# Order of steps in a hybrid attention, Mamba-2 and MLP block: outer SSM groups, one tile's transposes, the fifth up-projection unit

## The chip, the cores and the metric

The kernel runs on one core of a Trainium2 chip. The metric is the device time of one execution in microseconds; lower is better. The kernel before has a median of 1081.7 us in 3 runs (1081.41 to 1081.86).

## The reference

One decoder layer on 512 tokens of width 1024, all in float32. Cut to what matters:

```python
u = rmsnorm(h, norm_mix_pre_w)
q, k, v, z, xbc, dt_raw, gate_logits = split(u @ w_in)
att = dilated_attention(q, k, v) @ w_att_proj          # three (window, dilation) patterns, mixed
xs, bm, cm = split(silu(causal_conv4(xbc)))            # 8 groups of 256 channels, state 128
y = ssd_chunked(xs, dt, a, bm, cm) + d_skip * xs       # chunks of 128 tokens
y = group_rmsnorm(y * silu(z)) * ssm_norm_w            # one norm for each of the 8 groups
ssm = y @ w_ssm_proj
mixed = (sigmoid(g_att) * att + sigmoid(g_ssm) * ssm) @ w_out
h = h + rmsnorm(mixed, norm_mix_post_w)
f = square(relu(rmsnorm(h, norm_ffn_pre_w) @ w_up)) @ w_down    # hidden width 4096
h = h + rmsnorm(f, norm_ffn_post_w)
```

## The kernel before

Each float32 operand of a large product is split into a high part (`wh`, `uh`, `hh`, rounded for the matmul) and a low part (`wl`, `ul`, `hl`, the rest). ScalarE (ACT) makes the high part and VectorE (DVE) the low part. A product is then a triple of matmuls: high by high, high by low, low by high. Weights come in units of 1 MB (`ws_...`, two buffers), which the SP queue loads; a unit's load waits until the last reader of an older unit in the same buffer is done.

The order on TensorE (PE) is the order in which the program writes its matmuls. On the other engines a planner at build time sets the order by its own clock and by priorities; an instruction that is pinned stays behind the one written just before it on its engine. The planner's order is fixed in the program that runs.

**SSM groups.** The eight groups run one after the other (the loop at L923). The generator `ssm_group` (L791) has steps that hang together by short chains on several engines. In this order they are: scaling of the rows `xd` and `xs`; the products `pb` and `pcb` and the decays `w`, which DVE multiplies with `cbm`; the chunk states `pst` and `prev`; the outputs `pyd` and `pyo` with the gate, giving `y` and its square `sq`; the norm's sums `pn`, from which GpSimd (POOL) makes the power `rt` and sends it through DRAM (`rt_d`) back as a broadcast `rg`, and with which the next group's decays `w` are fetched; and the scaling of `y` by `rg`, split into `yth` and `ytl`, which the next projection reads (`pssp`). So that PE has work while these chains run, a `Filler` (L479) writes pieces of the large projections between the steps. One piece is one triple of 512 columns and counts 3 x 512 / 2400 = 0.64. The tuples `SSM_FIRST` (group 0), `SSM_FILL` (groups 1 to 6) and `SSM_LAST` (group 7) give the budget ahead of each of the seven steps; the sixth step is empty. What is overspent is taken from the next budget. The filling is a queue of units. In group 0 these are the attention projection, then `x` and `bc` of group 1. In groups 1 to 6 they are `z` of the group, the projection of the group before, then `x` and `bc` of the next group. In group 7 they are `z`, projection 6, and the gate units `gs1` to `gs3`; after these comes projection 7. When a unit's half (8 triples) ends, its evacuation is written with priority; for `x` of groups 1 to 7 that includes eight DMAs on the POOL queue, `x_d`, four for each half, and then `xd`.

**Output projection.** `out_right(i, j)` (L1013) is the second half of the output projection for token tile i: 4 triples for each of two halves j of the contraction, and after the second half `add_normed`, which gives the residual `hres`. `f_norm(i)` norms it into `fn`, and `f_transpose(i)` (L1029) transposes it on PE (`ft`) and splits it into `fh` and `fl`, which the up projection `up_first` reads.

**Up projection.** The first four units of 256 columns are plain products. Units 4 to 15 (the loop at L1245) are made by a Winograd form of Strassen's scheme: seven products of half size, with sums of the activations (`S1` to `S4`) and of the weights (`T1` to `T4`). The products are written in the order X (`A11`,`B11`), the previous unit's X (`S3`,`T3`), Y (`A12`,`B21`), the previous unit's Z (`S4`,`B22`), the previous unit's X (`A22`,`T4`), Z (`S1`,`T1`), X (`S2`,`T2`); each is 12 matmuls of 256 columns. `copy` moves a bank out on ACT (`usX`, `usY`, `usZ`), `c_sum` adds on DVE. The weight parts are split by `split_w` (L1170): ACT first, and the function that it returns does the DVE part. `b1_parts(j + 1)` splits `B11` and `B21` of the next unit (1024 columns), `b22_parts` splits `B22` (512 columns), `t12_parts` and `t34_parts` the sums, which `t_sums` (L1190) makes from the raw weights in `tt`. In the trace these tiles are `wh_wina`, `wl_wina` (for `B11`, `B21`, `T1`, `T2`) and `wh_winb`, `wl_winb` (`T3`, `T4`, `B22`). `load_up(j + 2)` (L1133) loads the raw weights of the unit after the next into the buffer of unit j. The fifth unit of the up projection is j = 4, where no previous unit of this kind exists; there the branch `else` splits `T3` and `T4`, `S3`, and `B22` of unit 4.

Of the kernel before, what the change touches and what calls it, by code (L numbers as in the profile page):

```python
# [42 lines left out]
BIG = 1e30  # L43

FILL0, FILL1, FILLA, FILLB, FILLC = 3.0, 4.0, 3.0, 2.8, 2.8
SSM_FIRST = (1, 5, 4, 3, 11, 5, 4.5)
SSM_FILL = (6, 4, 4, 4, 10, 5, 4.5)
SSM_LAST = (5, 6, 4, 4, 9, 8, 8)

V_ORDER = tuple((d, i) for d in (1, 0, 2) for i in range(NT))  # L50
V_STEPS = {(1, 0, 2): (("s", 2),), (1, 0, 5): (("t", 1),), (1, 0, 6): (("n", 2),), (1, 1, 1): (("s", 3),),
# [33 lines left out]
def hybrid_block(ctx: ExitStack, tc: tile.TileContext, a: dict):  # L85
# [77 lines left out]
    def v3(t, k):  # L163
        return t.rearrange("p (k n) -> p k n", k=k)
# [59 lines left out]
    def pin(ins):  # L224
        return tc.keep_in_program_order(ins)
# [4 lines left out]
    def tr(dst, src):  # L230
        tc.keep_in_program_order(pe.transpose(dst, src, ident))
# [4 lines left out]
    def three(ps, wh, wl, uh, ul, start, stop, w_moving=False):  # L236
        if w_moving:
            mm(ps, uh, wh, start=start, stop=False)
            mm(ps, uh, wl, start=False, stop=False)
            mm(ps, ul, wh, start=False, stop=stop)  # L240
        else:
            mm(ps, wh, uh, start=start, stop=False)
            mm(ps, wh, ul, start=False, stop=False)
            mm(ps, wl, uh, start=False, stop=stop)
# [11 lines left out]
    def gbank(name):  # L256
        return psg.tile([P, T], F32, name=name, tag="g")

    def abank(name):
        return psa.tile([P, T], F32, name=name, tag="a")  # L260
# [18 lines left out]
    with tc.tile_pool(name="start", bufs=1, reuse_waits="tile") as st:  # L279
# [7 lines left out]
        raw = st.tile([P, NT, SH], F32, name="dtraw")  # L287
# [341 lines left out]
    for key in ATT_UNITS:  # L629
        n, j = key[:-1], int(key[-1])  # L630
# [292 lines left out]
    for g in range(GROUPS):  # L923
        steps = ssm_group(g, szs[g])
        fill.through(f"bc{g}")
        for n, us in enumerate(SSM_FIRST if g == 0 else SSM_LAST if g == GROUPS - 1 else SSM_FILL):
            fill.run(us)
# [25 lines left out]
    w23 = []  # L953
    for j in range(2):
# [4 lines left out]
        lo = ow.tile([P, UF], F32R, name=f"wl_o{2 + j}", tag=f"ol{j}")  # L959
# [20 lines left out]
    def add_normed(i, pss, row, dst, at, parts=((0, T), (T, D))):  # L980

        ts_ = []
        for b in range(2):
            cs = slice(b * T, (b + 1) * T)
            jk = rp.tile([P, T], F32, name=f"jk{at}{i}_{b}", tag="jk", bufs=1)
            act.activation(jk, pss[b], AF.Square, scale=RD, accum_out=sm[:, at + b, i : i + 1])
            if b == 1:
                rstd_of(sm[:, at, i : i + 1], sm[:, at, i : i + 1], sm[:, at + 1, i : i + 1])
            t = rp.tile([P, T], F32, name=f"t{at}{i}_{b}", tag="jf", bufs=2)
            dve.tensor_tensor(t, pss[b], row[:, cs], op=ALU.mult)  # L990
            ts_.append(t)
        for c0, c1 in parts:
            tv = ts_[c0 // T][:, c0 % T : c0 % T + c1 - c0]
            dve.scalar_tensor_tensor(dst[:, c0:c1], tv, sm[:, at, i : i + 1], hres[:, i, c0:c1],
                                     op0=ALU.mult, op1=ALU.add)

    def out_part(ps, i, j, w, ks=range(4)):

        for k in ks:
            o = 4 * j + k  # L1000
            three(ps, v3(w[0], 4)[:, k, :], v3(w[1], 4)[:, k, :], mix[o][0][:, i * P : (i + 1) * P],
                  mix[o][1][:, i * P : (i + 1) * P], o == 0, o == KD - 1, w_moving=True)

    left = [abank(f"pso{i}") for i in range(NT)]
    right = [None] * NT
# [4 lines left out]
                out_part(left[i], i, j, w, ks)  # L1010
        done()

    def out_right(i, j):  # L1013
        if j == 0:
            right[i] = gbank(f"psp{i}")
        out_part(right[i], i, j, w23[j])
        if j == 1:
            add_normed(i, (left[i], right[i]), rowp, hres[:, i, :], 0)

    fn = {}  # L1020
# [1 line left out]
    def f_norm(i):  # L1022
        fn[i] = ow.tile([P, D], F32, name=f"fn{i}", tag="un", bufs=2)
        pin(act.activation(fn[i], hres[:, i, :], AF.Square, scale=RD, accum_out=sm[:, 2, i : i + 1]))
        pin(dve.tensor_scalar(sm[:, 3, i : i + 1], sm[:, 2, i : i + 1], EPS, None, ALU.add))
        pool.tensor_tensor(sm[:, 3, i : i + 1], sm[:, 3, i : i + 1], mhalf, op=ALU.pow)
        pin(dve.scalar_tensor_tensor(fn[i], hres[:, i, :], sm[:, 3, i : i + 1], rowf, op0=ALU.mult, op1=ALU.mult))

    def f_transpose(i):  # L1029
        for b in range(2):  # L1030
            pt = abank(f"ft{i}_{b}")
            for j in range(4):
                tr(pt[:, j * P : (j + 1) * P], fn[i][:, (4 * b + j) * P : (4 * b + j + 1) * P])
            p3 = pt.rearrange("p (k t) -> p k t", k=4)
            hi = fh[:, 4 * b : 4 * b + 4, i * P : (i + 1) * P]
            act.activation(hi, p3, AF.Copy)
            dve.tensor_tensor(fl[:, 4 * b : 4 * b + 4, i * P : (i + 1) * P], p3, hi.bitcast(F32), op=ALU.subtract)
# [16 lines left out]
    out_right(1, 1)  # L1054
    f_norm(1)
    out_right(2, 0)
    f_transpose(0)
    out_right(2, 1)
    out_right(3, 0)
    f_transpose(1)  # L1060
    f_norm(2)
# [30 lines left out]
    def blk(x, t, k):  # L1092
        return x[:, 4 * k : 4 * k + 4, HT * t : HT * t + HT]

    def scratch(n):
        return hid[:, 16 + 2 * n : 18 + 2 * n, :].rearrange("p a (b t) -> p (a b) t", t=HT)

    sm_["S3"] = [blk(fh, 1, 0), blk(fl, 1, 0)]
    A = {f"A{t + 1}{k + 1}": [blk(fh, t, k), blk(fl, t, k)] for t, k in ((0, 0), (0, 1), (1, 1))} | sm_
    raw = {f"A{t + 1}{k + 1}": scratch(2 * t + k) for t in range(2) for k in range(2)}  # L1100
# [8 lines left out]
    def split_s(n):  # L1109
        act.activation(A[n][0], raw[n], AF.Copy)  # L1110
        dve.tensor_tensor(A[n][1], raw[n], A[n][0].bitcast(F32), op=ALU.subtract)
# [54 lines left out]
    def quarter(n, j):  # L1166
        t, q = PLACE[n] if n != "B22" else (wb, 2 + j % 2)
        return [v3(x[:, q * T : (q + 1) * T], 4) for x in t]

    def split_w(dst, src):  # L1170
        hi, lo = dst
        pin(act.activation(hi, src, AF.Copy))
        return lambda: pin(dve.tensor_tensor(lo, src, hi.bitcast(F32), op=ALU.subtract))

    def b1_parts(j):
        return split_w([v3(x[:, : 2 * T], KD) for x in wa], v3(stages[j], KD)[:, :, :P])

    def b22_parts(j):
        return split_w(quarter("B22", j), v3(stages[j], KD)[:, 4:, P:])
# [31 lines left out]
    def bank(j, b):  # L1211
        return banks[j, b][:, :HT]

    def out_c(j, n, t):
        return hid[:, 2 * j + n, HT * t : HT * t + HT]

    def relu(x, src=None):
        with tc.high_priority(offset=0 if src is None else 400):
            pin(act.activation(x, x if src is None else src, AF.Relu))
# [6 lines left out]
    def copy(j, b):  # L1226
        us[j, b] = wp.tile([P, HT], F32, name=f"us{b}{j}", tag=f"us{b}", bufs=1)
        with tc.high_priority(offset=400):
            pin(act.activation(us[j, b], bank(j, b), AF.Copy))

    def c_sum(j, n, t, x, y):
        with tc.high_priority(offset=400):
            pin(dve.tensor_tensor(out_c(j, n, t), x, y, op=add))
# [11 lines left out]
    for j in WIN:  # L1245
        old, more = j > WIN[0], j < last
        if old:
            t_sums(j)
            copy(j - 1, "X")
        product(j, "X", "A11", "B11", True)  # L1250
        if old:
            lo = t12_parts()
            product(j - 1, "X", "S3", "T3", False)
            c_sum(j - 1, 1, 1, bank(j - 1, "X"), us[j - 1, "Z"])
            lo()
        else:
            t34_parts()()
            split_s("S3")
            b22_parts(j)()
        product(j, "Y", "A12", "B21", True)  # L1260
        load_up(j + 2)
        copy(j, "Y")
        c_sum(j, 0, 0, bank(j, "X"), us[j, "Y"])
        relu(out_c(j, 0, 0))
        lo = b1_parts(j + 1) if more else None
        if old:
            product(j - 1, "Z", "S4", "B22", False)
            c_sum(j - 1, 1, 0, us[j - 1, "X"], bank(j - 1, "Z"))
            relu(hid[:, 2 * j - 1, :])
            square(j - 1, 1)  # L1270
        if more:
            lo()
        if old:
            product(j - 1, "X", "A22", "T4", False)
            lo = t34_parts()
            relu(out_c(j - 1, 0, 1), bank(j - 1, "X"))
        product(j, "Z", "S1", "T1", True)
        copy(j, "Z")
        if old:
            lo()  # L1280
        if more:
            lo = b22_parts(j + 1)
        if old:
            square(j - 1, 0)
        product(j, "X", "S2", "T2", False)
        if more:
            lo()
        if j == last - 3:
            hs0 = [rp.tile([P, T], F32R, name=f"h{e}0", tag="jf", bufs=2) for e in "hl"]
            split_w(hs0, hid[:, 0, :])()  # L1290

    j = last
# [106 lines left out]
```

## Time and profile before

| | |
|---|---|
| median of 3 runs | 1081.7 us (1081.41 to 1081.86) |
| profiled execution, its own time | 1081.58 us |
| its span, first to last instruction | 1079.8 us |
| granted clock of TensorE, mean | 0.999 |
| chain that ended last | PE 89%, DVE 5%, ACT 2%, DMA 1% |
| memory | HBM read 113.59 MB, 111 GB/s over the span |

The span leaves out 1.8 us of the execution's own time. The chain that ended last is the chain of work followed back from the last instruction; the shares say on which engine it ran. In the timelines a row gives the start and the duration in us, the engine, the line, the operation, what it writes and reads, and in square brackets how long the engine was idle before it and what released it.

### The profile page before, as it was taken

The numbers are of one execution on the slowest core, as the hardware profiler recorded it, in microseconds if no ns is written. First come the engines' busy times: TensorE is split into PE (matmuls) and PEld (weight loads), VectorE is DVE, ScalarE is ACT, GpSimd is POOL, SyncE is SP. The second block draws the span as 40 slices with busy tenths as digits, with TensorE's granted clock in tenths as the row PEclk, the third lists the DMA queues.
The fourth block names the chain that finished last, engine by engine and source line by source line (L and its number), as shares of the span: only waits on it lengthen the run. The fifth ranks groups of instructions, "written<-read, shape, count | busy, mean of one in ns | idle before, by whom it ended". The sixth has DMA issues, their size and how long they took to land.

```text
span 1079.8 us, 14753 instructions
## 1 busy us (share of the span) xinstructions
PE 1068.1 (99%) x5903; PEld 909.2 (84%) x5903; DVE 741.7 (69%) x1103; ACT 534.6 (50%) x921; POOL 113.9 (11%) x150
## 2 busy tenths in 40 slices
PE   8999999999999999999999999999999999999997
PEld 8988888778878888888888878889899998888886
DVE  6657666436886889897989895878687785342324
ACT  6356656526374645547373733454466765322222
POOL 2203122000030211203030300010000000000000
PEclk9999999999999999999999999999999999999999
DMA  8232122222453544445454523540233324232202
GB/s 274 90 103 75 60 79 69 87 89 78 147 127 118 127 127 117 132 113 147 132 148 141 155 73 104 219 132 2 83 122 108 118 86 147 100 128 107 85 33 78
DMA packets 90454, 120.39 MB, mean 111 GB/s; under 512 B 5633, under 2 KB 75777, under 8 KB 89361
## 3 DMA queue, kind: packets, MB, share of 16 engines
q1 hardware_dynamic: 85216, 101.01, 29.4%
q0 software_dynamic: 5024, 18.44, 6.7%
q8 instruction: 46, 0.75, 0.3%
q14 instruction: 24, 0.19, 0.1%
q10 hardware_dynamic: 144, 0.00, 0.0%
HBM read 113.59 MB, written 5.85 MB: 111 GB/s over the span
## 4 chain that ended last, share of the span: by engine, by line
PE 89%; DVE 5%; ACT 2%; DMA 1%; issue 1%; POOL 0%; POOLq 0%; DVEq 0%; ACTq 0%
PE psd L228 16%; PE psx L228 8%; PE pssp L228 7%; PE psbc L228 7%; PE psz L228 7%; PE psuX L228 6%; PE psu L228 4%; PE psga L228 4%; PE psgs L228 4%; PE psv L228 3%; PE psk L228 3%; PE psq L228 3%; PE psap L228 3%; PE psuZ L228 3%; PE psuY L228 1%; PE pq L228 1%
## 5 line engine op out<-in xcount | busy, mean ns | idle before, releaser
L228 PE MATMUL psd<-wh_dn,hh 128*128 128x512 f32 x240 | 93.4, 389 | 0.0
L228 PE MATMUL psd<-wl_dn,hh 128*128 128x512 f32 x240 | 93.4, 389 | 0.0
L228 PE MATMUL psd<-wh_dn,hl 128*128 128x512 f32 x240 | 93.4, 389 | 0.0
L100 DVE TENSOR_TENSOR hl<-hidden,hh 128x512 fp32r<-128x512 f32 x31 | 21.1, 692 | 71.5 <-ACT hh L97 71.5
L97 ACT ACTIVATE hh<-hidden 128x512 fp32r<-128x512 f32 x31 | 19.1, 628 | 92.1 <-PE psd L228 92.1
L228 PEld LDWEIGHTS psd<-wh_dn,hl 128*128 128x128 f32 x240 | 45.1, 188 | 9.4
L228 PEld LDWEIGHTS psd<-wl_dn,hh 128*128 128x128 f32 x240 | 45.1, 188 | 9.4
L228 PEld LDWEIGHTS psd<-wh_dn,hh 128*128 128x128 f32 x240 | 45.1, 188 | 9.2
L228 PE MATMUL pssp<-yth,wh_sp 128*128 128x512 f32 x128 | 51.2, 400 | 0.1
L228 PE MATMUL pssp<-ytl,wh_sp 128*128 128x512 f32 x128 | 50.2, 392 | 0.7 <-DVE ytl L100 0.7
L228 PE MATMUL psx<-uh,wh_x 128*128 128x512 f32 x128 | 50.7, 396 | 0.0
L228 PE MATMUL pssp<-yth,wl_sp 128*128 128x512 f32 x128 | 50.2, 392 | 0.0
L228 PE MATMUL psz<-uh,wh_z 128*128 128x512 f32 x128 | 50.0, 391 | 0.0
L228 PE MATMUL psz<-uh,wl_z 128*128 128x512 f32 x128 | 49.9, 390 | 0.0
L228 PE MATMUL psx<-uh,wl_x 128*128 128x512 f32 x128 | 49.9, 389 | 0.0
L228 PE MATMUL psz<-ul,wh_z 128*128 128x512 f32 x128 | 49.8, 389 | 0.0
L228 PE MATMUL psx<-ul,wh_x 128*128 128x512 f32 x128 | 49.8, 389 | 0.0
L228 PE MATMUL psbc<-uh,wh_bc 128*128 128x512 f32 x128 | 49.8, 389 | 0.0
L228 PE MATMUL psbc<-ul,wh_bc 128*128 128x512 f32 x128 | 49.8, 389 | 0.0
L228 PE MATMUL psbc<-uh,wl_bc 128*128 128x512 f32 x128 | 49.8, 389 | 0.0
L694 DVE SCALAR_TENSOR_TENSOR ch<-psx,cw,ch 128x511 f32<-128x511 f32 (+2 forms) x48 | 35.9, 748 | 19.6 <-ACT ch L692 18.7
L97 ACT ACTIVATE wh_bc<-ws_bc 128x1024 fp32r<-128x1024 f32 x16 | 16.3, 1056 | 65.7 <-PE pssp L228 50.9
(365 smaller groups left out, 3292.0 us busy)
## 6 DMA issues: line engine op xcount, KB each, us to landing
ws_up<-in_w_up_dram SPq DMA_DIRECT2D x16, 1024.0 KB, 5.6
ws_dn<-in_w_down_dram SPq DMA_DIRECT2D x15, 1024.0 KB, 5.0
ws_z<-in_w_in_dram SPq DMA_DIRECT2D x8, 1024.0 KB, 7.7
ws_x<-in_w_in_dram SPq DMA_DIRECT2D x8, 1024.0 KB, 6.8
w<-acs_d POOLq DMA_DIRECT2D x8, 1024.0 KB, 5.6
ws_bc<-in_w_in_dram SPq DMA_DIRECT2D x16, 512.0 KB, 5.5
ws_sp<-in_w_ssm_proj_dram SPq DMA_DIRECT2D x8, 1024.0 KB, 5.0
ws_ga<-in_w_in_dram SPq DMA_DIRECT2D x4, 1024.0 KB, 5.5
```

The lines of the kernel that those rows point to most:

```text
L97: ins = act.activation(hi, src, AF.Copy)
L100: ins = (eng or dve).tensor_tensor(lo, src, hi.bitcast(F32), op=ALU.subtract)
L228: tc.keep_in_program_order(pe.matmul(*args, **kw))
L694: dve.scalar_tensor_tensor(h[:, d:], ps[:, : T - d], cw[:, ct, 3 - d : 4 - d], h[:, d:], op0=ALU.mult, op1=ALU.add)
```

## The change

Four orders change; no computation is added or taken away.

- `SSM_FIRST`: the fifth budget (ahead of the step with `pn`, group 0) goes from 11 to 9.5.
- `SSM_LAST`: the third and fourth budgets (ahead of `pst` and of `pyd`, group 7) go from 4 to 5, the seventh (ahead of the scaling) from 8 to 7.
- `out_right(2, 1)` is written in two parts of 2 triples, with `f_transpose(0)` between them instead of ahead of them.
- In the up projection's loop the ACT part of `b1_parts(j + 1)` is written ahead of the ReLU of the first quarter, in every unit; in unit 4 the splits of `S3` and `B22` move from behind the first product to behind the copy of Z, and the split of `S3` is now pinned.

```diff
-SSM_FIRST = (1, 5, 4, 3, 11, 5, 4.5)
+SSM_FIRST = (1, 5, 4, 3, 9.5, 5, 4.5)
 SSM_FILL = (6, 4, 4, 4, 10, 5, 4.5)
-SSM_LAST = (5, 6, 4, 4, 9, 8, 8)
+SSM_LAST = (5, 6, 5, 5, 9, 8, 7)
...
-    def out_right(i, j):
+    def out_right(i, j, ks=range(4)):
         if j == 0:
             right[i] = gbank(f"psp{i}")
-        out_part(right[i], i, j, w23[j])
-        if j == 1:
+        out_part(right[i], i, j, w23[j], ks)
+        if j == 1 and 3 in ks:
             add_normed(i, (left[i], right[i]), rowp, hres[:, i, :], 0)
...
     out_right(2, 0)
+    out_right(2, 1, range(2))
     f_transpose(0)
-    out_right(2, 1)
+    out_right(2, 1, range(2, 4))
     out_right(3, 0)
...
             t34_parts()()
-            split_s("S3")
-            b22_parts(j)()
         product(j, "Y", "A12", "B21", True)
         load_up(j + 2)
         copy(j, "Y")
         c_sum(j, 0, 0, bank(j, "X"), us[j, "Y"])
+        lo = b1_parts(j + 1) if more else None
         relu(out_c(j, 0, 0))
-        lo = b1_parts(j + 1) if more else None
...
         copy(j, "Z")
         if old:
             lo()
+        else:
+            split_w(A["S3"], raw["S3"])()
+            b22_parts(j)()
         if more:
             lo = b22_parts(j + 1)
```

## Rows read from the trace of the kernel before

**Rows 1.** The page's busy time: us, share of the span, instructions.

```profile
PE 1068.1 (99%) x5903; PEld 909.2 (84%) x5903; DVE 741.7 (69%) x1103; ACT 534.6 (50%) x921; POOL 113.9 (11%) x150
```

**Rows 2.** Waits of PE: who waited for whom, us, times, longest.

```profile
PE pyd L228 <- DVE w L829: 1.0, 2, 0.8
PE pssp L228 <- DVE ytl L100: 0.7, 1, 0.7
PE psuX L228 <- DVE wl_wina L1173: 0.5, 1, 0.5
```

**Rows 3.** The chain in order of time: start, us, instructions; group 3.

```profile
433.37 2.02 PE pyd L228 x32
...
439.01 8.84 PE psx L228 x39
```

**Rows 4.** Timeline of PE, group 0's output projection, in group 1.

```profile
322.28 0.40 PE L228 MATMUL pssp<-yth,wl_sp 128*128 128x512 f32 x1
...
323.95 0.50 PE L228 MATMUL pssp<-ytl,wh_sp 128*128 128x512 f32 x1 [0.65 <-DVE ytl L100]
```

**Rows 5.** Timeline of PE, group 7's states and outputs.

```profile
629.17 0.28 PE L228 MATMUL pst<-xsl,bkh 128*128 128x256 f32 x1
629.55 0.39 PE L228 MATMUL pst<-xsh,bkl 128*128 128x256 f32 x1
...
634.70 0.66 PE L228 MATMUL pyd<-w,xd 128*64 128x128 f32 x8
...
638.00 1.27 PE L228 MATMUL pyo<-ct,prev 128*128 128x128 f32 x9
```

**Rows 6.** Timeline of PE, the first tile's transposes.

```profile
720.06 0.39 PE L228 MATMUL psp<-wh_o,ml 128*128 128x512 f32 x1
720.82 1.06 PE L231 MATMUL ft<-ident,fn 128*128 128x128 f32 x8 [0.37 <-DVE sm L215]
```

**Rows 7.** Timeline of PE, up projection: unit 5's X, then unit 5's X with S3.

```profile
783.25 0.28 PE L228 MATMUL psuX<-fl,wh_wina 128*128 128x256 f32 x1
784.00 0.39 PE L228 MATMUL psuX<-fh,wl_wina 128*128 128x256 f32 x1 [0.48 <-DVE wl_wina L1173]
...
795.38 0.28 PE L228 MATMUL psuX<-fh,wh_winb 128*128 128x256 f32 x1
```

**Rows 8.** Timeline of POOL: group 0 (first three rows) and group 1.

```profile
304.93 2.57 POOL L745 DMA_DIRECT2D x_d<-sqt  x4 [3.61 <-DVE sqt L742]
307.52 1.06 POOL L216 TENSOR_TENSOR rt<-rt,mhalf 128x4 f32<-128x4 f32 x1
...
310.94 0.55 POOL L888 DMA_DIRECT2D rg<-rt_d  x1 [0.37 <-DMA rt_d<-rt]
...
349.14 1.04 POOL L216 TENSOR_TENSOR rt<-rt,mhalf 128x4 f32<-128x4 f32 x1 [12.85 <-DVE rt L213]
...
358.81 0.57 POOL L888 DMA_DIRECT2D rg<-rt_d  x1
```

**Rows 9.** Instructions on tile rg, all eight groups: from issue to landing, us.

```profile
DMA to landing us min/median/max: 3.7/3.8/6.9
```

**Rows 10.** Timeline of DVE: the last two decays of group 7.

```profile
635.42 1.29 DVE L829 TENSOR_TENSOR w<-w,cbm 128x512 f32<-128x512 f32 x2
```

**Rows 11.** Timeline of ACT, up projection, units 4 and 5.

```profile
780.45 0.38 ACT L1229 ACTIVATE usY<-psuY 128x256 f32<-128x256 f32 x1 [1.03 <-PE psuY L228]
...
781.64 1.04 ACT L1172 ACTIVATE wh_wina<-ws_up 128x1024 fp32r<-128x1024 f32 x1
...
789.64 1.04 ACT L1172 ACTIVATE wh_wina<-ws_up 128x1024 fp32r<-128x1024 f32 x1
...
794.29 0.38 ACT L1229 ACTIVATE usX<-psuX 128x256 f32<-128x256 f32 x1
```

**Rows 12.** Waits of the SP queue, 740 to 850 us: us, times, longest.

```profile
SPq L1138 <- DVE wl_winb L1173: 19.9, 1, 19.9
```

**Rows 13.** The page's DMA issues: count, KB each, us to landing.

```profile
ws_up<-in_w_up_dram SPq DMA_DIRECT2D x16, 1024.0 KB, 5.6
```

## The prediction

> **What bounds the kernel now.** I read the page's busy shares first: TensorE (PE) is busy 99% of the span [rows 1], so only time in which PE stands still can be won. Then the waits of PE alone: apart from start-up there are the wait of `pyd` for the decays `w`, of `pssp` for `ytl` (once, although eight groups run that code), of `psuX` for `wl_wina` [rows 2], and a fourth, of the transposes `ft`, given below. Each lies beside one edit, so I looked at each place in the timeline, from start to start. The pace comes from the chain: 39 matmuls of 512 columns take 8.84 us, 0.227 us each [rows 3], so 0.68 for a triple (one unit of filling) and about 0.12 for 256 columns.
>
> - Group 0's output projection: 322.28 to 323.95 with one matmul between, 1.67 instead of 0.46: **1.21 us** lost [rows 4].
> - Last group: 629.17 to 629.55 is 0.38 instead of 0.12, 0.26 lost; `pyd` starts at 634.70 and `pyo` at 638.00, 3.30, where the same 32 matmuls take 2.02 in another group [rows 3, 5], 1.28 lost: **1.54** together.
> - `ft`: 720.06 to 720.82, 0.76 instead of 0.23: **0.53** [rows 6].
> - `psuX`: 783.25 to 784.00, 0.75 instead of 0.12: **0.63** [rows 7].
>
> Together 3.91 us, the most that can be won here.
>
> The waits of these places, as the profile shows them, add up to only 2.5 us (0.65, 1.0, 0.37, 0.48 [rows 2, 4, 6, 7]); taken at that, the gains would be 1.4 us smaller. The Trainium skill (Perfetto Trace Analysis, section "Tensor Engine Instruction (MATMUL, LD_WEIGHTS)") says why I don't use them: a matmul's reported end is estimated from its size, so idle time counted from it is short. The traced starts here agree (1.21 against 0.65).
>
> **Part 1, the first group's budget (11 to 9.5).** A triple costs 0.64 in the filler's currency. The old budgets put 17 triples between the step with `pyd` and the one with `pn` (the norm's sums); the new ones 15, then 7 and 7 instead of 8 and 7. So `pn` comes 2 triples earlier (1.36 us) and the scaling step 3 earlier. No instruction is added. What decides is GpSimd's queue. In group 0 the power `rt` stands at 307.52, behind the row DMAs `x_d` of the unit's second half (304.93 to 307.50), and so the broadcast `rg` goes out at 310.94. In group 1, where the budgets put `pn` 9 matmuls before the second half of `x` ends instead of 6, the power is at 349.14, ahead of those DMAs, and `rg` follows behind them at 358.81 [rows 8]; groups 2 to 6 repeat this. With 12 matmuls left, group 0 should take group 1's order: `rg` at about 307.5, 3.4 us earlier. Landing takes 3.7 to 6.9 us [rows 9], thus 311.2 to 314.4 instead of 317.8 at its slowest; `ytl` is 1.2 us late, so 3.4 us suffices. This step's other DMAs (`rt_d`, the decays' broadcast `w`) go out no later than now; `x_d` of the first half can slip by one power, 1.06 us [rows 8], which the second half's wait of 3.61 takes up. Gain: 1.21 if the order turns, 0 if not; a loss is unlikely since the other groups run the new order without this wait. I take **-1.2**.
>
> **Part 2, the last group's budgets.** In triples: (8, 10, 6, 6, 15, 12, 13) becomes (8, 10, 7, 8, 15, 12, 11). The state sums move 1 triple later, the `pyd` step and the norm step 3, the final scaling 1. The 0.26 is covered by 0.68 of work. At `pyd`, PE now arrives at 634.70 - 0.26 + 2.04 = 636.48, and VectorE ends the last two decays at 636.71 today [rows 5, 10]; they are not the first that `pyd` reads, so about nothing is left. But VectorE is full there: 3 more triples finish projection unit 6 before `pyd`, so one more accumulation (0.65 from two 512-column operations in 1.29 [rows 10]) can get ahead of the decays; then the last two reach PE 0.65 late and I keep only 0.9. Bounds: 0.9 to 1.54 gained, with the loss under the rivals. Behind it, the norm step stands at the same absolute time to 0.5 us, and the last projection 1.5 us earlier: 32 triples, 21.8 us, after `pn`. Group 0's chain from the power to `ytl` took 16.4 us with a slow DMA [rows 4, 8], so that cover holds. I take **-1.5**.
>
> **Part 3, one tile's transposes.** They move behind 6 matmuls of 512 columns, 1.36 us, against a wait of 0.53 [rows 6]. Nothing is issued anew; the additions still follow the last part. What is late next: the second tile's transposes come 0.53 us sooner while their input hangs on VectorE and not on PE. Bounds 0 to 0.53; I take **-0.5**.
>
> **Part 4, the up projection's fifth unit.** Two things change. ScalarE splits the next unit's `B1` quarters ahead of a ReLU that waits for VectorE, in every unit; and in the first such unit the splits of `S3` and of `B22` move from before the second product to behind the third one's copy.
> The gain: the split now starts at 781.64, directly behind that ReLU; it can start when the copy that began at 780.45 is out, 780.83 at the latest [rows 11]. That is 0.8 us earlier, against a wait of 0.63. So the 0.63 goes.
> The loss has two terms. (a) On ScalarE the order from 780.8 is `B1` (1.04), ReLU and copy of Z (0.38 each or less), `S3` (1.04), two `B22` splits (half as wide, some 0.55) and the copy of X (0.38): 4.3 us, less some 0.1 of overlap at each of the six joints, so the copy of X is out near 784.6 to 784.7 (estimate from [rows 11]). The next product into that bank is due at 783.13 + 12 x 0.12 = 784.57: 0.1 of wait. (b) SP. The buffers of raw weights are two, and the load of unit 6 waited for `wl_winb`, the low half of this very `B22`, as SP's waits show (once, 19.9 us [rows 12]; for later units the last reader is a sum in `tt`). The low halves now follow each other on VectorE: `B1` to 783.1 (1.2 behind its high half, out at 781.9), `S3` to 784.5 (its high half is out at 783.3), `B22` to 785.2 (512 columns 0.65 [rows 10], 1024 columns 1.2 by that). Landing takes 5.6 us [rows 13]: 790.8. But the split of unit 6's `B1` started at 789.64 [rows 11], and would start before 789.3 in the new order. ScalarE stands still until 790.8 with everything behind it. From that split to the next copy of X are 4.65 us now (789.64 to 794.29 [rows 11]), plus the ReLU that moved behind it (0.3 to 0.4, as wide as the copies of 0.38): the copy begins at 795.8 and is out at 796.2. The product that needs it started at 795.38 [rows 7]; without the 0.63 and with (a) it is due at 794.85: **1.3 us** of wait. Later loads have slack, since they hang on `tt` as before, so this is paid once; the earlier split gives later units some room and costs PE nothing, as it has no wait there now. Bounds: -0.5 (no waiting for the load) to +1.1. Sum -0.63 + 0.1 + 1.3 = **+0.8**.
>
> **Sum.** -1.2 - 1.5 - 0.5 + 0.8 = -2.4. The profiled execution took 1081.58 (span 1079.8 and 1.8 around it), 0.1 under the median 1081.7; so 1079.2 by its own scale and 1079.3 against the median.
>
> **Rivals.**
> 1. The load doesn't hold ScalarE up (the raw buffer comes free some other way). For it: every later load leaves long before its use, so the load alone was no limit. Against: SP's wait names that very operation [rows 12]. Then part 4 gives -0.5: -3.7, 1078.0. Chance 0.14.
> 2. In the last group an accumulation gets ahead of the decays, and the gain there is 0.9 or less. For it: VectorE is the late one there, and accumulations have precedence in the code. Against: its input comes 1.36 us after the one before, which is time for two decays. 1079.9 to 1080.3. Chance 0.20.
> 3. The change doesn't do what it says in group 0: the planner leaves the power behind the row DMAs. Then -1.2 falls away: 1080.5. For it: the order is the planner's, on its own clock. Against: group 1's order under a similar budget [rows 8]. Chance 0.10.
> 4. Slower. The end of projection unit 6 now comes before `pyd`, and with it the splits of a gate unit's weights, which have precedence (two of 1.04 on ScalarE, two of 1.2 on VectorE). If these get ahead of the last two decays on VectorE, they start only when PE has left that projection (634.70 - 0.26 + 1.36 = 635.8), and the decays end near 640.6 (1.04 and two of 1.2 and 1.29 later): PE waits 3.9 us instead of 1.54, a loss of 2.4 in place of 1.5 gained. 1081.7 - 1.2 + 2.4 - 0.5 + 0.8 = 1083.2. It decides as soon as the planner has the splits ready before the last decay but one. Against: without a wait that decay starts at about 635.2, before ScalarE has the first half. Chance 0.07.
>
> **How the numbers follow.** The forecast has 0.49, with its own range 1078.8 to 1079.8. What a measurement can tell from no change is 0.2%, 2.2 us, so the border is 1079.5: some seven tenths of the forecast (0.34) and rival 1 lie below it, 0.48 in all; rest of the forecast, rivals 2 and 3 give 0.45; rival 4 0.07. The range 1077.8 to 1080.7 holds the forecast and rivals 1 to 3 except their tails, and leaves out rival 4.
>
> **What would show it.** Right: GpSimd's power ahead of the `x_d` rows of unit 1's second half, and no wait of `pssp` for `ytl`; `pyd` in about 2.0 us in the last group; no gap before the first `ft`; SP's load of up-projection unit 6 leaving near 785 in the old time scale, ScalarE idle before the split of its weights, and a PE wait of about 1.3 us for the copy `usX`, one unit later. Wrong: that wait missing, or a wait for `w` in the last group over 0.7 us.

## The result, and the profile after

The changed kernel took **1084.0 us** (median of 17 runs, 1082.15 to 1085.62), the kernel before, run beside it, 1081.86 (17 runs, 1081.41 to 1082.38). The ratio is 1.0019, 95% interval [1.0012, 1.0026]: 0.19% slower, where 0.2% faster was predicted. The profiled execution of the changed kernel (1082.15, span 1080.4) is the shortest of its 17, so some of what makes the others longer is not in its trace; a second profile of the same kernel, below, has it. Lines from 1016 on are one number higher than before.

First the waits of PE (who waited for whom, us, times, longest), against [rows 2]:

```profile
PE pyd L228 <- DVE w L829: 2.8, 2, 2.7
...
PE psuX L228 <- ACT usX L1230: 1.2, 1, 1.2
```

The wait of `pssp` for `ytl` is gone, as is the one of `psuX` for `wl_wina`, and the one of `ft` for `sm`. A wait for the copy `usX` is new, which was forecast. The wait of `pyd` was to vanish and has grown from 1.0 to 2.8. The timeline of PE there (start, us, instruction, idle before it), against [rows 5]:

```profile
635.18 0.66 PE L228 MATMUL pyd<-w,xd 128*64 128x128 f32 x8
638.49 0.44 PE L228 MATMUL pyd<-w,xd 128*64 128x128 f32 x4 [2.66 <-DVE w L829]
639.10 1.31 PE L228 MATMUL pyd<-w,xd 128*64 128x128 f32 x20 [0.16 <-DVE w L829]
640.34 1.60 PE L228 MATMUL pyo<-ct,prev 128*128 128x128 f32 x12
641.70 0.48 PE L228 MATMUL psgs<-uh,wh_gs 128*128 128x512 f32 x1
```

From `pyd` to `pyo` are 5.16 us, where the same 32 matmuls take 2.02 in another group [rows 3] and took 3.30 before [rows 5]. That is 1.86 more, or **1.60** after taking off the 0.26 that PE no longer loses at the states. From start to start the two waits are 2.87 and 0.38, **3.25 us**; this count takes 1.91 for the matmuls themselves, and by it the waits of `pyd` before were 1.39. The prediction's 1.28 takes 2.02 for them, as group 3 does, and is 0.1 lower. Why they are late is in VectorE's timeline of the same stretch, against [rows 10]:

```profile
634.18 0.69 DVE L829 TENSOR_TENSOR w<-w,cbm 128x512 f32<-128x512 f32 x1
634.79 0.68 DVE L730 TENSOR_TENSOR acc<-acc,pssp 128x512 f32<-128x512 f32 x1
635.48 2.36 DVE L100 TENSOR_TENSOR wl_gs<-ws_gs,wh_gs 128x1024 fp32r<-128x1024 f32 x2
637.75 1.29 DVE L829 TENSOR_TENSOR w<-w,cbm 128x512 f32<-128x512 f32 x2
```

The last accumulation of projection unit 6 and then two splits of a gate unit's weights stand ahead of the last two decays. The decays start at 637.75, 2.3 us later than before, while PE arrives half a microsecond later. That is rival 4. The decays were not waiting for their own input: `cbm` was out at 629.5 and ScalarE's last pass over `w` at 609.4.

The other two places that carry the sum. GpSimd in group 0, against [rows 8]:

```profile
296.81 1.05 POOL L216 TENSOR_TENSOR rt<-rt,mhalf 128x4 f32<-128x4 f32 x1 [11.74 <-DVE rt L213]
...
298.77 2.63 POOL L745 DMA_DIRECT2D x_d<-sqt  x4
305.04 2.56 POOL L745 DMA_DIRECT2D x_d<-sqt  x4 [3.64 <-DVE sqt L742]
307.60 0.58 POOL L888 DMA_DIRECT2D rg<-rt_d  x1
```

The power is now ahead of both halves of `x_d`, and `rg` goes out at 307.60 instead of 310.94. And the up projection, first on PE, then on ScalarE, against [rows 7, 11]:

```profile
794.62 0.28 PE L228 MATMUL psuX<-fh,wl_wina 128*128 128x256 f32 x1
796.06 0.39 PE L228 MATMUL psuX<-fh,wh_winb 128*128 128x256 f32 x1 [1.16 <-ACT usX L1230]
```

```profile
780.62 1.05 ACT L1173 ACTIVATE wh_wina<-ws_up 128x1024 fp32r<-128x1024 f32 x1
...
790.65 1.06 ACT L1173 ACTIVATE wh_wina<-ws_up 128x1024 fp32r<-128x1024 f32 x1 [1.71 <-DMA ws_up<-in_w_up_dram]
...
795.62 0.38 ACT L1230 ACTIVATE usX<-psuX 128x256 f32<-128x256 f32 x1
```

ScalarE stands 1.71 us for the load of unit 6, and the copy behind it lets PE stand: 796.06 - 794.62 - 0.12 = 1.32 us. SP's wait for the low half of `B22`, 19.9 us before [rows 12], is 24.2:

```profile
SPq L1139 <- DVE wl_winb L1174: 24.2, 1, 24.2
```

For this execution the terms are -1.21 (group 0), +1.60 (last group), -0.53 (`ft`) and 1.32 - 0.63 = +0.69 (up projection): +0.55, and its span is 0.6 longer than that of before (1080.4 against 1079.8). The median, however, is 2.1 longer. The experiments had to find 1.5 us more.

### The profile page after: what moved, and what is told of

The parts are those of the page before. It is cut to its first block, busy times and chain, and to the rows that moved or that the text cites. A ratio compares the mean times of both kernels' runs of the same rounds, so it can differ in the third digit from the quotient of the medians.

```text
span 1080.4 us, 14749 instructions
## 1 busy us (share of the span) xinstructions
PE 1067.6 (99%) x5903; PEld 909.8 (84%) x5903; DVE 740.6 (69%) x1103; ACT 535.5 (50%) x921; POOL 114.8 (11%) x150
## 4 chain that ended last, share of the span: by engine, by line
PE 95%; DMA 2%; DVE 1%; ACT 1%; issue 1%; SPq 0%; POOLq 0%; POOL 0%; DVEq 0%; ACTq 0%
PE psd L228 16%; PE psx L228 8%; PE psz L228 8%; PE psbc L228 8%; PE pssp L228 8%; PE psuX L228 5%; PE psu L228 4%; PE psga L228 4%; PE psgs L228 4%; PE psk L228 3%; PE psap L228 3%; PE psq L228 3%; PE psv L228 3%; PE psuZ L228 3%; PE psp L228 2%; PE pso L228 2%
```

## The experiments

Theory A: part 2 alone makes it slower, by the order of VectorE in the last group (rival 4). Rival B: the loss comes from the load in part 4, or from several small waits. Of the runs that follow, the first four share one set of runs of the kernel before (median 1081.86, 31 runs), the next four another (1081.81, 26 runs), the last two a third (1081.64, 12 runs).

**The changed kernel once more**, without an edit, for a second profile.

> The changed kernel once more, unaltered, for a second profile. Theory A (the wait of pyd for the last two decays in the last group, 2.87 + 0.38 us from start to start, is what lets the granted TensorE clock fall in most executions): median 1084.0 +- 0.4, granted clock 0.997, and if this profile is not one of the short ones, a stretch behind 638 us in which the granted clock is at the lower level, worth about 2 us. Rival B (the longer executions have a longer wait somewhere else, such as the load of up-projection unit 6): the clock is 1.00 until 1040 us and one of the waits is some 2 us longer than in the first profile.

1084.08 (11 runs), ratio 1.0021 [1.0012, 1.0030]. This time the profiled execution, 1084.88, is among the longer ones. The table by stretches, one microsecond each: its length, PE's busy time and instructions, the granted clock, and the DMAs' share and rate:

```profile
638.00:639.00 1.00, 0.00 (x0) 1.00 0.00 0
639.00:640.00 1.00, 0.62 (x6) 0.51 0.22 70
640.00:641.00 1.00, 1.00 (x12) 0.50 0.57 168
641.00:642.00 1.00, 1.00 (x14) 0.50 1.06 430
642.00:643.00 1.00, 1.00 (x9) 0.78 0.92 373
643.00:644.00 1.00, 1.00 (x10) 1.00 0.08 25
```

```profile
639.38 3.00 PE L228 MATMUL pyd<-w,xd 128*64 128x128 f32 x24 [2.65 <-DVE w L829]
642.31 1.65 PE L228 MATMUL pyo<-ct,prev 128*128 128x128 f32 x12
643.72 0.48 PE L228 MATMUL psgs<-uh,wh_gs 128*128 128x512 f32 x1
```

PE has stood for 2.65 us, and when it starts again at 639.38 the granted clock is 0.50, the lower level (1.2 of 2.4 GHz); the first row back at 1.00 is the one from 643. From the first `pyd` matmul behind the wait to the gate unit's matmul are 4.34 us; in the first profile, at 1.00 throughout, the same stretch took 3.21 (638.49 to 641.70). So the clock costs **1.1 us** on top of the wait. The Trainium skill (TensorE: Matmul & The Clock Gate, section "What's actually happening") says that in the kernels measured there the gate had two ratios only, half and full. The rows agree: they show 0.50 and 1.00, and 0.51 and 0.78 only where the clock falls and comes back. Two other waits are longer than in the first profile: that for `usX`, 1.60 instead of 1.32 from start to start, and a new one:

```profile
PE psu L228 <- DVE fl L1037: 0.3, 1, 0.3
```

From start to start it is 0.43 us. It comes from part 3, and is taken up with that step.

**Part 2 alone.** The kernel before with this edit:

```diff
-SSM_LAST = (5, 6, 4, 4, 9, 8, 8)
+SSM_LAST = (5, 6, 5, 5, 9, 8, 7)
```

> The kernel before with the new budgets of the last group alone. Theory A: the wait ahead of pyd grows from 1.54 us (with the states') to about 3.25, +1.7 us by the sum of waits, and with the lower clock behind it 1.9 more in most executions: 1085.4 +- 0.6, clock 0.997, executions spread over 1 to 3 us. Rival B (the spread comes from another of the four edits): 1083.6, clock 0.998 to 0.999, spread under 1 us. The prediction's own step would give 1080.4.

1084.43 (9 runs), ratio 1.0023 [1.0013, 1.0032]: part 2 by itself is as slow as the whole change, 1 us less than was expected of it. The wait is there again, and so is the clock, at 0.50 from 640 to 642 us:

```profile
PE pyd L228 <- DVE w L829: 2.7, 1, 2.7
```

**The change without part 2**: the line above turned back, all else as changed.

> The changed kernel with the old budgets of the last group; the other three edits stay. Theory A: -1.21 (group 0) - 0.53 (ft) + 0.68 (1.31 us of new wait for usX, 0.63 of old wait gone) = -1.06: 1080.8 +- 0.4, no lower clock, spread under 1 us. Rival B: the spread and the lower clock stay, about 1082.5.

1081.03 (11 runs), ratio 0.9994 [0.9986, 1.0003], 3.0 us under the changed kernel. `pyd` waits as before, and the clock is 1.00 throughout that stretch:

```profile
PE pyd L228 <- DVE w L829: 1.0, 2, 0.8
PE psu L228 <- DVE fl L1037: 0.3, 1, 0.3
```

**The splits without precedence.** The changed kernel, budgets and all, but the second gate unit's splits lose their offset, so that the planner has no reason to put them ahead of the decays:

```diff
-    ... in ("x", "bc", "z", "sp") or key == "o1" else offset)
+    ... in ("x", "bc", "z", "sp") or key in ("o1", "gs2") else offset)
```

> The changed kernel in which the weight splits of gate unit 2 have no precedence, so that VectorE does the last two decays ahead of them; the budgets stay new. Theory A: the last decay but one starts where the first split started, 635.5, instead of 637.75; pyd waits about 0.95 us instead of 3.25, so 2.3 us less than the short executions and no lower clock: 1079.9 +- 0.4. Rival C (the pyd step is late for another reason, its place behind projection 6 or the accumulations): the wait stays over 2 us and the time near 1084.

1080.27 (11 runs), ratio 0.9986 [0.9977, 0.9995], 3.8 us under the changed kernel with the same budgets. VectorE's timeline:

```profile
634.36 0.68 DVE L829 TENSOR_TENSOR w<-w,cbm 128x512 f32<-128x512 f32 x1
634.96 0.68 DVE L730 TENSOR_TENSOR acc<-acc,pssp 128x512 f32<-128x512 f32 x1
635.56 1.29 DVE L829 TENSOR_TENSOR w<-w,cbm 128x512 f32<-128x512 f32 x2
636.76 1.22 DVE L100 TENSOR_TENSOR wl_gs<-ws_gs,wh_gs 128x1024 fp32r<-128x1024 f32 x1
```

The two decays are ahead of the split, and end at about the time at which they ended before [rows 10]. PE's waits there are 0.50 and 0.38, 0.88 together. So the budgets themselves are good: by the medians this run is 0.8 under the one with the old budgets. The place of the splits costs 2.4 us of waiting (3.25 against 0.88) and the clock behind it (1.1 by the traces above, 1.4 by the run that follows), together 3.5 to 3.8.

By the order in the trace, what is left, 0.88, is due to two other instructions that now stand ahead of the last two decays: one accumulation more (six instead of five between the split of `xs` and these decays), which is rival 2, and a gate's part of the sum (L901). The latter stood behind them in the kernel before, and stands ahead of all four here. First the row of before, then that of the changed kernel; this run has it in the same place, at 629.59:

```profile
636.62 0.68 DVE L901 SCALAR_TENSOR_TENSOR acc<-gst,acc 128x512 f32<-128x512 f32 x1
```

```profile
629.40 0.68 DVE L901 SCALAR_TENSOR_TENSOR acc<-gst,acc 128x512 f32<-128x512 f32 x1
```

Each takes 0.60 us from start to start. Counted from the split of `xs` on VectorE, the last two decays start 1.2 us later than before; rival 2 said 0.65.

**PE kept busy.** The changed kernel with 12 matmuls of 512 columns ahead of the last group's `pyd`, whose result is overwritten:

```diff
         pyds = [abank(f"pyd{g}_{j}") for j in range(2)]
+        if g == GROUPS - 1:
+            for _ in range(12):
+                mm(pyds[0], bk[0][:, :P], xsp[0][:, :T], start=True, stop=True)
```

> The changed kernel with 12 matmuls of 512 columns ahead of the last group's pyd, whose result pyd overwrites (12 x 0.227 = 2.72 us, about the stretch in which PE stood, 636.4 to 639.4). The decays are as late as before. Theory A (the granted clock falls because PE stands there): the clock stays 1.00 from 636 to 644, pyd reaches pyo at the same time as in the changed kernel, and the time is that kernel's less the 1.9 us that the slow matmuls cost: 1082.2 +- 0.5, its shortest execution. Rival B (the clock falls from something else in this stretch, or the 1.9 us have another cause): 0.50 again behind pyd, 1084.1.

1082.67 (11 runs), ratio 1.0009 [1.0000, 1.0018]: 2.7 us of useless work make the kernel 1.4 faster. Timeline of PE, then its clock:

```profile
635.51 2.89 PE L228 MATMUL pyd<-xsh,bkh 128*128 128x512 f32 x12
638.33 1.02 PE L228 MATMUL pyd<-w,xd 128*64 128x128 f32 x12
639.52 1.31 PE L228 MATMUL pyd<-w,xd 128*64 128x128 f32 x20 [0.16 <-DVE w L829]
640.76 1.49 PE L228 MATMUL pyo<-ct,prev 128*128 128x128 f32 x11
```

```profile
640.00:641.00 1.00, 1.00 (x18) 1.00 0.90 348
641.00:642.00 1.00, 1.00 (x11) 1.00 1.03 418
```

The decays come as late as in the changed kernel, and `pyo` starts as late (640.76 against 640.34; the 0.4 us between them are there from the first 40 us on), but the clock stays at 1.00. The mean granted clock of all 11 executions is 0.998 or 0.999, where the longer ones of the changed kernel have 0.996 to 0.998. It was the standing still that cost the clock, and that price is 1.1 (traces) to 1.4 us (medians), less than the 1.9 that the expectation took from the shortest and the median time.

**Part 4 alone**: the kernel before with the edits of the up projection only.

> The kernel before with part 4 alone (the up projection's fifth unit). Theory A (the load of unit 6 waits for the low half of B22 and lands late): wait for wl_wina (0.63) gone, wait for usX of 1.3 to 1.6 one unit later, 1081.86 + 0.7 to 1.0 = 1082.7. Rival B (the load is innocent; the usX wait comes from the other parts' earlier arrival): no usX wait, 1081.2. The granted clock stays 1.00 around pyd in the last group either way.

1082.28 (11 runs), ratio 1.0006 [0.9998, 1.0015]: 0.5 longer, which the medians alone hardly tell from nothing. The trace does, in two rows of the timeline, 795.98 - 794.62 - 0.12 = 1.24:

```profile
794.62 0.28 PE L228 MATMUL psuX<-fh,wl_wina 128*128 128x256 f32 x1
795.98 0.39 PE L228 MATMUL psuX<-fh,wh_winb 128*128 128x256 f32 x1 [1.09 <-ACT usX L1229]
```

**B22 left ahead of the load.** The splits without precedence, and of part 4 only `B1` and `S3` moved:

```diff
             t34_parts()()
+            b22_parts(j)()
         product(j, "Y", "A12", "B21", True)
         load_up(j + 2)
...
             split_w(A["S3"], raw["S3"])()
-            b22_parts(j)()
```

> The changed kernel with the second gate unit's splits without precedence, and with unit 4's B22 splits left ahead of the load (S3 alone moves). Theory A: the load of unit 6 leaves at its old time, the usX wait of 1.44 goes, the other waits stay: 1080.3 - 1.4 = 1078.9 +- 0.5. Rival B (B1 ahead of the ReLU or the moved S3 is what makes the copy late): the usX wait stays, 1080.3.

1078.71 (7 runs), ratio 0.9973 [0.9962, 0.9984], 1.6 less than with `B22` behind the load. The `usX` wait is gone, and SP waits for `wl_winb` as long as before [rows 12]:

```profile
SPq L1139 <- DVE wl_winb L1174: 19.9, 1, 19.9
```

So moving `B22` past the load was all of part 4's loss; `B1` ahead of the ReLU and the later `S3` open no new wait in this trace, and the 0.63 for `wl_wina` does not come back.

**Two decays with precedence**, on top of that:

```diff
-            dve.tensor_tensor(wv, wv, cbm...)
+            with tc.high_priority(offset=250 if g == GROUPS - 1 and c >= 2 else 0):
+                dve.tensor_tensor(wv, wv, cbm...)
```

> best2 with the last group's third and fourth decays given precedence over the accumulations too. The two waits ahead of pyd (0.50 and 0.38 in split_later) shrink to 0.2 to 0.5 together: 1078.9 - 0.5 = 1078.4. Rival: the accumulations or the states that go behind the decays become the late ones (pssp's bank, or pyo waiting for prev): 1078.9 or above.

1078.81 (8 runs), ratio 0.9973 [0.9963, 0.9983]: no better. The two waits of 0.50 and 0.38 have become one of 1.06 from start to start:

```profile
635.56 0.44 PE L228 MATMUL pyd<-w,xd 128*64 128x128 f32 x4
636.84 1.75 PE L228 MATMUL pyd<-w,xd 128*64 128x128 f32 x28 [0.84 <-DVE w L830]
```

PE now stops after 4 instructions and not after 8: the decays with precedence went first, and the last to be ready is the second that `pyd` reads. The miss is mine: I gave precedence to those that came last, not to those that are needed first.

**Part 3 undone**, in the kernel with `B22` ahead of the load:

```diff
-    out_right(2, 1, range(2))
     f_transpose(0)
-    out_right(2, 1, range(2, 4))
+    out_right(2, 1)
```

> best2 with tile 0's transposes where the kernel before has them (part 3 undone). Theory A (part 3 trades one wait for another of the same size): the wait of ft is back (0.13 to 0.53 in the runs that have it), the wait of psu for fl (0.23 in best2) is gone, 1078.7 + 0.0 to 0.3. Rival B (part 3 is worth the 0.5 that was predicted): 1079.2.

1078.89 (8 runs) against 1078.71, ratio to before 0.9973 [0.9963, 0.9983]; the two can't be told apart by time. In the trace the wait of `ft` is 0.59 from start to start, and that of `psu` for `fl`, 0.23, is gone:

```profile
718.39 0.39 PE L228 MATMUL psp<-wh_o,ml 128*128 128x512 f32 x1
719.21 0.95 PE L231 MATMUL ft<-ident,fn 128*128 128x128 f32 x7 [0.43 <-DVE sm L215]
```

**More work ahead of `pyd`**, again on top of `B22` ahead of the load. The expectation counts one more triple; it is two. The fourth budget, 6.4, is 10 pieces of 0.64, where 5 gave 8, and nine `psgs` matmuls stand ahead of `pyd` instead of three. The budgets behind it are smaller by the same two triples:

```diff
-SSM_LAST = (5, 6, 5, 5, 9, 8, 7)
+SSM_LAST = (5, 6, 5, 6.4, 8.5, 8, 6)
```

> best2 with one more triple ahead of the last group's pyd, SSM_LAST (5, 6, 5, 6.4, 8.5, 8, 6): PE reaches pyd 0.68 later, against waits of 0.50 and 0.38. Theory A: the two waits shrink to 0.2 to 0.4 together and nothing else moves, 1078.7 - 0.6 = 1078.1. Rival B (VectorE takes as much more work ahead of the decays as PE does, as in part 2): the waits stay, 1078.7.

**1077.79** (5 runs, 1077.58 to 1077.89), ratio 0.9964 [0.9950, 0.9977]: 0.36% under the kernel before, the fastest of all. In the last group PE no longer waits:

```profile
634.42 0.39 PE L228 MATMUL psgs<-uh,wh_gs 128*128 128x512 f32 x1
...
636.24 0.39 PE L228 MATMUL psgs<-uh,wl_gs 128*128 128x512 f32 x1
636.55 1.97 PE L228 MATMUL pyd<-w,xd 128*64 128x128 f32 x32
638.45 1.60 PE L228 MATMUL pyo<-ct,prev 128*128 128x128 f32 x12
```

VectorE's rows in the same stretch:

```profile
634.80 0.68 DVE L730 TENSOR_TENSOR acc<-acc,pssp 128x512 f32<-128x512 f32 x1
635.40 1.29 DVE L829 TENSOR_TENSOR w<-w,cbm 128x512 f32<-128x512 f32 x2
```

Here the two triples put nothing more ahead of the decays on VectorE: its order there is that of the run with `B22` ahead of the load, and their 1.36 us cover the 0.88 of waiting. Whether one triple alone would have left a part of the wait, as the expectation has it, was not run. The gain is 0.9 by the medians, 0.75 if each run is set against its own runs of the kernel before.

## Why the prediction was wrong, step by step

**Part 1, right** in mechanism and size. The power turned ahead of `x_d`, `rg` left 3.3 us earlier, and all 1.21 us came back. No run has this part alone; the wait of `pssp` for `ytl` stands in both profiles without it (part 2 alone, part 4 alone) and in none of the nine with it.

**Part 2 is the step that failed.** The prediction put "I take -1.5" on the claim that little of the wait is left since VectorE "ends the last two decays at 636.71". They ended at 639.0, and the part cost 1.6 of waiting and 1.1 to 1.4 of clock, 2.7 to 3.0 in place of -1.5; by the medians it is 2.6 (part 2 alone against before) and 3.0 (the changed kernel with and without it). The mechanism was written down as rival 4, with the right instructions. Its price, a wait of 3.9, does not follow from its own times: if the decays end at 640.6 and `pyo` starts 1.29 us behind their end, as in [rows 5, 10], PE loses 3.4 against the pace of group 3, and 3.14 were measured by that count. What was wrong was its chance, 0.07, and the argument for it: that the decay could start "before ScalarE has the first half" of the weights. That is an argument from chip times, and they came out nearly so: next in the order, the decays would have started 0.60 us behind the accumulation, as in the run without the precedence, so at 635.39, and the splits started at 635.48. But the order on VectorE is fixed by the planner before anything runs, by its own estimates and by precedence. On the chip the decays' input was there, and VectorE did the splits first all the same, in both profiles of the changed kernel. The difference between the changed kernel and the one without the precedence shows it, with budgets that are the same. No rival priced the clock: in the trace of before it is at 1.00 around each of the waits that the prediction dealt with. So even rival 4's time, 1083.2, was 0.8 under the median, and would have been lower still with its own wait of 3.4.

**Part 3, half right.** The wait of `ft` went, but a new one came that the sum put at nothing. Of the second tile's transposes the prediction said that "their input hangs on VectorE and not on PE", and it followed that no further. With the transposes later, VectorE does both halves of tile 0's `fl` behind the norm of tile 1, and tile 1's `fl` comes when PE wants to read it. That wait was 0.43, 0.46 and 0.38 us in the three profiles of the first group of runs that have part 3, 0.34, 0.23 and 0.19 in three later ones, and under 0.1 in two, the first profile among them. The wait that part 3 removes varies as well: 0.53 in the profile of before, but 0.13 and 0.23 in the profiles with part 2 alone and with part 4 alone, and 0.59 in the last comparison. A term read from one execution was taken as fixed. What part 3 is worth is the difference of two such waits, by these figures between a loss of 0.3 us and a gain of 0.6. The run with part 3 undone has 0.2 for it by the medians, and 0.35 if each run is set against its own runs of the kernel before, both within the noise; so its worth is not shown.

**Part 4, right**: the old wait went, the load left late for the reason that SP's row named, and PE paid 1.24 to 1.7 where 1.3 was predicted. Term (a), 0.1, did not show as a wait. Rival 1 is out, by the run with `B22` ahead of the load.

**Rival 3** did not happen. **Rival 2** did, once rival 4 was taken out of the way, together with the gate's sum that it did not name: the 0.88 left in the last group.

With the clock's 1.1, the new wait for `fl` and the longer wait for `usX`, the second profile's terms are -1.3 (group 0), +2.7 (last group, from 600 to 680 us), -0.1 (transposes) and +1.0 (up projection): +2.3, against 2.1 to 2.2 between the medians. That execution's own time is 1 us longer still, from its first 40 us, in which PE stands 3.8 us against 2.7 in the profile of before.

## What to carry to other kernels

When PE's budget of filling work moves, ask what the other engines' planner now finds ready earlier, and which of it has precedence over the work that PE waits for: the order of their queues is fixed before the chip has a say, so a forecast of it needs the planner's order and not the trace's times. A long wait of PE can cost more than its length, so a change that may open one should be priced with the slower clock behind it. Here two parts were spoilt by one group of instructions on the wrong side of another (weight splits ahead of decays, a split behind the load that waits for its buffer); put right, and with two more triples of cover, the same change made the kernel 0.36% faster.

## What was not expected of the hardware

- After 2.65 us in which PE stood still, the granted clock was at 0.50 when it started again, and back at 1.00 from 643, in two of three traces with this wait; in the third, with a wait of 2.66, it stayed at 1.00. Waits of 1.0 to 1.7 us (for `ytl`, `w` and `usX`) left it at 1.00 wherever I looked. The same stretch filled with matmuls whose result is overwritten kept it at 1.00. What decides between the two outcomes of the same wait stays open.
- The wait of `ft` for the sum of squares' scale (0.13 to 0.59) and the time that PE stands in the first 40 us (2.3 to 3.8) vary between executions with the same code in that place; a gain of half a microsecond that rests on such a wait is one execution's.
